# Seven block products over four PSUM banks in a decoder trunk, and memory probabilities in another pool

## The chip, the cores and the metric

The kernel runs on one core of a Trainium2 chip. The metric is the device time of one execution in microseconds (us). Engines: PE (TensorE, matmuls), DVE (VectorE), ACT (ScalarE), POOL (GpSimd) and SP (SyncE, which here only issues DMAs). SBUF is the on-chip memory; PSUM has eight banks, each 128 x 512 float32, which matmuls write.

## The reference

Four decoder layers over 256 tokens of width 1024, all in float32:

```python
def reference(x, mem, ...):
    mem_n = _rmsnorm(mem, g_mem)
    for i in range(DEPTH):                      # DEPTH = 4
        proj = _rmsnorm(x, g_mix[i]) @ w_in[i]  # 1024 -> 3 * 1024 + 256
        cols, mq = proj[..., :3 * MIX_WIDTH], proj[..., 3 * MIX_WIDTH:]
        mix = ...                               # i % 3: stick-breaking attention,
                                                # differential attention, short gated convolution
        mo = _memory_attention(mq, mem_n, w_mem_kv[i])   # 4 heads x 64, 256 memory tokens, softmax
        x = x + jnp.concatenate([mix, mo], axis=-1) @ w_o[i]
        x = x + _swiglu(_rmsnorm(x, g_ffn[i]), w_ffn_in[i], w_ffn_out[i])
    return _rmsnorm(x, g_final)

def _swiglu(x, w_in, w_out):
    gu = x @ w_in                               # 1024 -> 2 * 2816
    return (jax.nn.silu(gu[..., :D_FF]) * gu[..., D_FF:]) @ w_out
```

## The kernel before

All weights (225 MB) are streamed once. The 256 tokens are two tiles of 128 (t = 0, 1). A weight matrix comes in chunks of 128 x 1024 numbers: `wchunk` issues one DMA on SyncE into a *raw* tile (pool `wraw`, 7 tiles), and `wparts` splits it: ACT casts it into `whi` (L131, a shorter float format that PE runs in one pass), and DVE writes what the cast lost into `wlo` (L132). Both live in the pool `wsplit`, eight of each. The tokens are split in the same way (`xth`, `xtl`), so a product is three matmuls, `mm3` (L136 to L138). They have 128 x 128 weights loaded in PE (of the tokens) and 512 moving columns (of the chunk).

`proj` takes a projection of 512 columns: four chunks, for each t 24 matmuls into one PSUM bank, and then an evacuation. `out_proj` does the output projections with four banks. Work that has to follow some time later is put into a list by `later(rounds, f)`, and `flush()`, called in the middle and at the end of each pass over a chunk set, runs what is due. So the Python order of the program weaves the attention of one projection into the matmuls of the next one.

The order on each engine is made by a planner: it takes the instructions by their place in the program, lets one go ahead when what it needs is ready in the planner's own model of the time, and gives out the tiles of a pool. Tiles with one tag share that tag's buffers. At run time each engine follows its list in order and waits on semaphores.

Memory attention (`mem_attention`, one for each layer) runs in `first`, `second` and `third`: `probs(0)` on the first token tile (12 matmuls L383, maximum L386, exponentials L390 on ACT, scaling L394 on DVE), then `turn(0)` (transposes L402, copies L406 and L408) and `probs(1)`, then `turn(1)` and `values`. In layer 0 this lies in the second mixer half's first projection, in the others in the first mixer half's second and third. The probabilities `mprob` (128 x 4 x 256 floats) take a tile of `wraw`, as large as a weight chunk.

The feed-forward input projection has six blocks (b = 0 to 5): gate columns and up columns of 512 each, the last with 256 each. Blocks 0, 2, 3 and 5 are plain `proj` calls. Blocks 1 and 4 use `winograd`: with the tokens (two halves of the width, two token tiles) and the weights (two halves of the rows; gate and up) as 2 x 2 blocks, seven block products take the place of eight. Products 1 and 2 use plain weight and token blocks; 5, 6, 7 and 4 use sums of weight blocks (`plus`, L221 on DVE, `wsum` or in place in a raw tile); 5, 7, 6 and 3 use sums of token blocks, which `tokens_side` makes once for each layer after block 0 (L256 to L262, split in L252 and L253). A product needs four row chunks, two in each of two rounds s = 0, 1. Each of the seven has a PSUM bank of its own through both rounds, and in the second round `h_sums` combines them on DVE (L859 to L873), applies SiLU on ACT (L860, L874) and multiplies gate and up (L852). `hidden` then transposes the result (L836) into the operand `hh`, `hl` of the output projection.

The tag `att` of the pool `work` has NATT = 12 tiles of 128 x 512 floats, for attention, the tokens' sums and the products' sums. `small` has four one-column tiles for each tag.

Of the kernel before, what the change touches and what calls it, by code (L numbers as in the profile page):

```python
# [32 lines left out]
NATT = 12  # L33
# [7 lines left out]
def trunk_kernel(ctx, tc, x, mem, vecs, w_in, w_kv, w_o, w_f1, w_f2, lams, g_final, out):  # L41
# [3 lines left out]
    wraw = pool("wraw", 7)  # L45
# [151 lines left out]
    def winograd(left, right, ab, evac):  # L197
# [99 lines left out]
    def rstd_of(ss, n, scale, eps):  # L297

        r = small.tile([P, n], F32, name="rstd", tag=f"rstd{n}")
        nc.gpsimd.tensor_scalar(r, ss, scale, eps, ALU.mult, ALU.add)  # L300
        nc.gpsimd.tensor_tensor(r, r, nhalf[:, :n], ALU.pow)
        return r

    def stats(src):
        junk = work.tile([P, D], BF16, name="junk", tag="att", bufs=NATT)
        ss = small.tile([P, 1], F32, name="ss", tag="ss")
# [61 lines left out]
    def mem_attention(qT, kv):  # L368
# [5 lines left out]
        def probs(t):  # L374
            prob = wraw.tile([P, 4, S], F32, name="mprob", tag="raw")
            mx = small.tile([P, 4], F32, name="mmx", tag="mmx")
            sm = small.tile([P, 4], F32, name="msm", tag="msm")
# [7 lines left out]
            for r, ps in enumerate(pss):  # L385
                nc.vector.tensor_reduce(mx[:, 2 * r:2 * r + 2], ps, AX.X, ALU.max)  # L386
                nc.vector.tensor_scalar(mx[:, 2 * r:2 * r + 2], mx[:, 2 * r:2 * r + 2], -0.125, None, ALU.mult)
                for pr in range(2):
                    j = 2 * r + pr
                    nc.scalar.activation(prob[:, j, :], ps[:, pr, :], AF.Exp, bias=mx[:, j:j + 1], scale=0.125,  # L390
                                         accum_out=sm[:, j:j + 1])
            nc.vector.reciprocal(sm, sm)
            for j in range(4):
                nc.vector.tensor_scalar(prob[:, j, :], prob[:, j, :], sm[:, j:j + 1], None, ALU.mult)  # L394
            return prob

        def turn(t, prob):
            for j0 in (0, 2):
                tr = ps_x.tile([P, 4, P], F32, name="tr", tag="ps")
                for j in (j0, j0 + 1):  # L400
                    for m in range(NT):
                        nc.tensor.transpose(tr[:, 2 * (j - j0) + m, :], prob[:, j, m * P:(m + 1) * P], ident)  # L402
# [98 lines left out]
    def diff_scores(qT, kT, hh0, lam, res, then):  # L501
        diffs = []
        abias = alibi(hh0)
        for e in range(2):
            bias = abias[:, e]
            mx = small.tile([P, 4], F32, name="dmx", tag="dmx")
            sm = small.tile([P, 4], F32, name="dsm", tag="dsm")
# [36 lines left out]
    def diff_values(aTs, v, c0, oh, ol, ghead):  # L544
        ons = []
        for e in range(2):
# [7 lines left out]
            ss = small.tile([P, 2], F32, name="dss", tag="dss")  # L554
# [35 lines left out]
    def final():  # L590
        gfin = big.tile([P, D], F32, name="gfin", tag="big")
        nc.sync.dma_start(gfin, g_final.partition_broadcast(P))
        ss = [small.tile([P, 2], F32, name="fss", tag="fss") for _ in range(NT)]
# [83 lines left out]
    for i in range(DEPTH):  # L677
# [29 lines left out]
        def q_scale(t):  # L707
            r = small.tile([P, 1], F32, name="rq", tag="rq")
# [105 lines left out]
        for b in range(6):  # L814
# [29 lines left out]
            if b in (1, 4):  # L844
                sums = {}

                def h_sums(p, acc, sums=sums, sg=sg, hh=hh, hl=hl):
                    tt = nc.vector.tensor_tensor
                    new = lambda name: work.tile([P, 512], F32, name=name, tag="att", bufs=NATT)

                    def up(t, c):
                        nc.vector.scalar_tensor_tensor(sg[t], c, rneg[t], sg[t], ALU.mult, ALU.mult)  # L852
                        later(2, lambda: hidden(t, sg[t], hh, hl, 512))

                    if p == 1:
                        sums["v"] = new("sv")
                        nc.scalar.copy(sums["v"], acc[1])
                    elif p == 2:
                        tt(sg[0], acc[2], sums["v"], ALU.add)  # L859
                        nc.scalar.activation(sg[0], sg[0], AF.Silu, scale=rx[0])  # L860
                    elif p == 6:
# [68 lines left out]
```

## Time and profile before

| | |
|---|---|
| median of 3 runs | 1333.34 us (1332.73 to 1334.71) |
| profiled execution: time, span | 1336.26 us, 1334.5 us |
| mean granted TensorE clock in it | 0.986 of full |
| instructions | 16363, of which 6079 matmuls |
| weights read | 225.23 MB, mean 170 GB/s over the span |
| DMAs of feed-forward input weights | 160 of 512 KB, median 4.3 us to landing |

The span is the time from the first to the last instruction; the profiled execution's own time has 1.8 us around it. An instruction's row names the engine, the line, the operation and `out<-in` by the names of the tiles. "[4.41 <-ACT whi L131]" says that the engine had been idle for 4.41 us and that the end of ACT's instruction on `whi` at line 131 released it. Rows of a list of waits read: who waits, for whom, us in total, times, the longest. "x5" merges neighbours of one kind, from the start of the first to the end of the last. SPq is SyncE's issuing of a DMA; PEld is the loading of PE's 128 x 128 operand, which overlaps the matmuls.

### The profile page before, as it was taken

To read this page: it belongs to the slowest core of one execution; us is meant where nothing else is said; L and a number is where in the kernel's file an instruction comes from. 1 tells how busy PE (TensorE), PEld (TensorE's weight loads), DVE (VectorE), ACT (ScalarE), POOL (GpSimd) and SP (SyncE) were. 2 spreads that over 40 slices of the span, in tenths; PEclk is the share of its full clock that TensorE was granted. 3 is DMA by queue.
4 is the path that set the end of the run, shared out by engine and by line. 5 is a ranking of instruction groups with operands and counts; after the bars stand their busy time and mean duration, and the time that the engine had idled before them with its cause. 6 is when DMAs were issued, how large, how long until landed. Compare 5 with 4: busy or idle time off the path is not lost.

```text
span 1334.5 us, 16363 instructions
## 1 busy us (share of the span) xinstructions
PE 1290.3 (97%) x6079; PEld 1056.6 (79%) x6079; DVE 930.3 (70%) x1163; ACT 721.1 (54%) x1015; POOL 60.0 (4%) x109
## 2 busy tenths in 40 slices
PE   9989999999989999999998999999999899999997
PEld 6878887878878888787886888788888688878786
DVE  7645598795647659879464877978744745996952
ACT  7646466564446546656344545656434655664642
POOL 2000000000111000000000000000000001000001
PEclk9989999999999999999998999999999899999999
DMA  9426536477426454747743664475752645364660
GB/s 342 149 74 211 158 112 224 135 226 243 121 84 207 172 158 122 242 124 242 221 126 103 224 196 124 140 240 161 263 171 79 205 142 158 88 213 156 202 224 31
DMA packets 107791, 227.34 MB, mean 170 GB/s; under 512 B 7488, under 2 KB 20288, under 8 KB 107712
## 3 DMA queue, kind: packets, MB, share of 16 engines
q1 hardware_dynamic: 107712, 226.31, 52.9%
q8 instruction: 47, 0.77, 0.2%
q14 instruction: 32, 0.26, 0.1%
HBM read 225.23 MB, written 1.05 MB: 170 GB/s over the span
## 4 chain that ended last, share of the span: by engine, by line
PE 76%; DVE 16%; issue 3%; ACT 2%; DMA 1%; SPq 0%; POOL 0%; POOLq 0%; ACTq 0%; DVEq 0%
PE acc L137 23%; PE acc L138 23%; PE acc L136 23%; DVE wlo L132 7%; DVE wsum L221 2%; ACT whi L131 1%; PE tr L334 1%; DMA raw<-in_w_ffn_out 1%; PE tr L836 1%; PE tr L320 1%; DVE raw L221 1%; DVE sl L253 1%; PE at L415 1%; PE at L449 1%; PE at L491 1%
## 5 line engine op out<-in xcount | busy, mean ns | idle before, releaser
L132 DVE TENSOR_TENSOR wlo<-raw,whi 128x1024 fp32r<-128x1024 f32 (+1 forms) x428 | 510.0, 1209 | 186.1 <-ACT whi L131 183.1
L131 ACT CAST whi<-raw 128x1024 fp32r<-128x1024 f32 (+1 forms) x428 | 436.9, 1042 | 277.0 <-PE acc L138 215.5
L136 PE MATMUL acc<-whi,xth 128*128 128x512 f32 (+1 forms) x992 | 396.5, 400 | 18.0 <-ACT whi L131 17.6
L137 PE MATMUL acc<-wlo,xth 128*128 128x512 f32 (+1 forms) x992 | 388.0, 391 | 13.4 <-DVE wlo L132 13.4
L138 PE MATMUL acc<-whi,xtl 128*128 128x512 f32 (+1 forms) x992 | 385.5, 389 | 0.0
L136 PEld LDWEIGHTS acc<-whi,xth 128*128 128x128 f32 x992 | 189.6, 191 | 56.1 <-ACT whi L131 20.1
L137 PEld LDWEIGHTS acc<-wlo,xth 128*128 128x128 f32 x992 | 189.8, 191 | 54.1 <-DVE wlo L132 20.1
L138 PEld LDWEIGHTS acc<-whi,xtl 128*128 128x128 f32 x992 | 189.6, 191 | 37.8
L136 PE MATMUL acc<-whi,hh 128*128 128x512 f32 x320 | 125.4, 392 | 0.0
L138 PE MATMUL acc<-whi,hl 128*128 128x512 f32 x320 | 124.6, 389 | 0.0
L137 PE MATMUL acc<-wlo,hh 128*128 128x512 f32 x320 | 124.5, 389 | 0.0
L131 ACT CAST whi<-wsum 128x1024 fp32r<-128x1024 f32 x48 | 50.5, 1052 | 55.8 <-DVE wsum L221 52.0
L138 PEld LDWEIGHTS acc<-whi,hl 128*128 128x128 f32 x320 | 60.1, 188 | 12.5
L137 PEld LDWEIGHTS acc<-wlo,hh 128*128 128x128 f32 x320 | 60.1, 188 | 12.2
L136 PEld LDWEIGHTS acc<-whi,hh 128*128 128x128 f32 x320 | 60.1, 188 | 12.2
L132 DVE TENSOR_TENSOR wlo<-wsum,whi 128x1024 fp32r<-128x1024 f32 x48 | 58.5, 1218 | 5.9 <-ACT whi L131 5.5
L137 PE MATMUL acc<-wlo,sh 128*128 128x512 f32 x128 | 50.7, 396 | 0.7
L136 PE MATMUL acc<-whi,oh 128*128 128x512 f32 x128 | 51.1, 399 | 0.0
L138 PE MATMUL acc<-whi,ol 128*128 128x512 f32 x128 | 50.0, 391 | 0.0
L138 PE MATMUL acc<-whi,sl 128*128 128x512 f32 x128 | 49.9, 390 | 0.0
L137 PE MATMUL acc<-wlo,oh 128*128 128x512 f32 x128 | 49.9, 390 | 0.0
L136 PE MATMUL acc<-whi,sh 128*128 128x512 f32 x128 | 49.2, 389 | 0.0
(215 smaller groups left out, 1415.0 us busy)
## 6 DMA issues: line engine op xcount, KB each, us to landing
raw<-in_w_ffn_in SPq DMA_DIRECT2D x160, 512.0 KB, 4.3
raw<-in_w_in SPq DMA_DIRECT2D x100, 512.0 KB, 4.4
raw<-in_w_ffn_out SPq DMA_DIRECT2D x88, 512.0 KB, 4.8
raw<-in_w_o SPq DMA_DIRECT2D x40, 512.0 KB, 4.6
raw<-in_w_mem_kv SPq DMA_DIRECT2D x16, 512.0 KB, 5.4
raw<-in_w_ffn_in SPq DMA_DIRECT2D x32, 256.0 KB, 3.6
raw<-in_w_in SPq DMA_DIRECT2D x8, 256.0 KB, 5.6
x<-in_x SPq DMA_DIRECT2D x4, 256.0 KB, 4.2
```

The source lines that it names most:

```text
L131: nc.scalar.copy(hi, raw)
L132: wlast[:] = [nc.vector.tensor_tensor(lo, raw, hi.bitcast(F32), ALU.subtract)]
L136: nc.tensor.matmul(ps, lh, wh, start=first, stop=False)
L137: nc.tensor.matmul(ps, lh, wl, start=False, stop=False)
L138: return nc.tensor.matmul(ps, ll, wh, start=False, stop=last)
L221: nc.vector.tensor_tensor(out, a, b, ALU.add)
L253: tt(lo, src, hi.bitcast(F32), ALU.subtract)
L320: last_pe = nc.tensor.transpose(ps[:, c, :], src[:, kc * P:(kc + 1) * P], ident).ins
L334: nc.tensor.transpose(ps[:, c, :], src[:, c * P:(c + 1) * P], ident)
L415: nc.tensor.matmul(ps[r * 64:(r + 1) * 64, 0, :], vn[:, m, c:c + 64], pT[2 * r + pr][:, m, :], start=m == 0, stop=m == NT - 1)
L449: nc.tensor.matmul(z[:, 0:2, :], kT[:, h, 0:P], qT[:, h, :], start=True, stop=True)
L491: nc.tensor.matmul(ps[:, 0:2, :], v[0][:, c:c + P], a[h][:, 0:2, :], start=True, stop=False)
```

## The change

Four things change.

1. `winograd` becomes `strassen`. The seven products run in two parts: products 1, 5, 7 and 6 for both rounds, and then 2 for both rounds, and 4 and 3 by turns. They share four banks: 1 and 2, 5 and 3, 7 and 4 accumulate in one bank each, 6 has its own. The sums with 6 and 1 (`u`) and with 7 (`y`) are read off the banks between the two parts. The weight sums of both rounds and the raw chunks b22 are kept until the second part, which also loads b21. `gated` takes over from `h_sums`: the gate half of t = 0 goes from PSUM straight to SiLU, the three others add `u` or `y` to what is in PSUM.
2. `tokens_side` and the negated scales are called between the gate and the up projection of block 0, not after both.
3. `mprob` is two tiles of the tag `att` (2 x 256 floats each) and no longer a raw tile. `wraw` has 8 tiles, `att` 11.
4. Small one-column tiles of several tags share one tag with 14 buffers.

```diff
-NATT = 12
+NATT = 11
...
-    wraw = pool("wraw", 7)
+    wraw = pool("wraw", 8)
...
-    def winograd(left, right, ab, evac):
+    def strassen(left, right, ab, out):
         acc = {}
+        banks = {1: 1, 2: 1, 5: 5, 3: 5, 7: 7, 4: 7, 6: 6}
         def product(p, w, s):
-            if s == 0:
-                acc[p] = ps_acc.tile([P, 512], F32, name="acc", tag="ps")
+            b = banks[p]
+            if b not in acc:
+                acc[b] = ps_acc.tile([P, 512], F32, name="acc", tag="ps")
             lh, ll = ab[p]
             for k in range(2):
                 kc = 2 * s + k
-                mm3(acc[p], lh[:, kc, :], ll[:, kc, :], w[0][:, k, :], w[1][:, k, :], kc == 0, kc == 3)
-            if s == 1:
-                evac(p, acc)
+                start, stop = kc == 0 and p == b, kc == 3
+                nc.tensor.matmul(acc[b], lh[:, kc, :], w[0][:, k, :], start=start, stop=False, skip_group_check=True)
+                nc.tensor.matmul(acc[b], lh[:, kc, :], w[1][:, k, :], start=False, stop=False, skip_group_check=True)
+                nc.tensor.matmul(acc[b], ll[:, kc, :], w[0][:, k, :], start=False, stop=stop, skip_group_check=True)
...
+        part = lambda name: work.tile([P, 512], F32, name=name, tag="att", bufs=NATT)
+        b22, sums = [], []
+        v, u, y = part("sv"), part("su"), part("sy")
         for s in range(2):
             b11, b12 = (load(c, 2 * s * P) for c in (left, right))
-            b21, b22 = (load(c, 512 + 2 * s * P) for c in (left, right))
+            b22.append(load(right, 512 + 2 * s * P))
             product(1, wparts(b11), s)
             t = wraw.tile([P, 2, 512], F32, name="wsum", tag="raw")
             plus(t, b11, b12)
+            if s == 1:
+                nc.scalar.copy(v, acc[1])
             product(5, wparts(t), s)
             flush()
-            product(2, wparts(b21), s)
-            plus(t, t, b22)
+            plus(b12, b12, b22[s])
+            product(7, wparts(b12), s)
+            plus(t, t, b22[s])
             product(6, wparts(t), s)
             flush()
-            plus(b12, b12, b22)
-            product(7, wparts(b12), s)
-            product(3, wparts(b22), s)
+            sums.append(t)
+        plus(u, acc[6], v)
+        plus(y, acc[7], u)
+        b21 = [load(left, 512 + 2 * s * P) for s in range(2)]
+        for s in range(2):
+            product(2, wparts(b21[s]), s)
+        out(0, 0, acc[1], None)
+        out(1, 1, acc[5], y)
+        flush()
+        for s in range(2):
+            plus(sums[s], sums[s], b21[s])
+            product(4, wparts(sums[s]), s)
+            if s == 1:
+                out(1, 0, acc[7], u)
+            product(3, wparts(b22[s]), s)
             flush()
-            plus(t, t, b21)
-            product(4, wparts(t), s)
+        out(0, 1, acc[5], u)
...
-            prob = wraw.tile([P, 4, S], F32, name="mprob", tag="raw")
-            mx = small.tile([P, 4], F32, name="mmx", tag="mmx")
-            sm = small.tile([P, 4], F32, name="msm", tag="msm")
+            probs2 = [work.tile([P, 2, S], F32, name="mprob", tag="att", bufs=NATT) for _ in range(2)]
+            prob = [probs2[j // 2][:, j % 2, :] for j in range(4)]
+            mx = small.tile([P, 4], F32, name="mmx", tag="sm", bufs=14)
+            sm = small.tile([P, 4], F32, name="msm", tag="sm", bufs=14)
...
-                def h_sums(p, acc, sums=sums, sg=sg, hh=hh, hl=hl):
...
+                def gated(t, side, ps, add, sg=sg, hh=hh, hl=hl, up={}):
+                    if side == 0:
+                        src = ps
+                        if add is not None:
+                            nc.vector.tensor_tensor(sg[t], ps, add, ALU.add)
+                            src = sg[t]
+                        nc.scalar.activation(sg[t], src, AF.Silu, scale=rx[t])
+                        up[t, 0] = sg[t]
+                    else:
+                        up[t, 1] = add if t == 1 else work.tile([P, 512], F32, name="sx", tag="att", bufs=NATT)
+                        nc.vector.tensor_tensor(up[t, 1], ps, add, ALU.add)
+                    if (t, 0) in up and (t, 1) in up:
+                        nc.vector.scalar_tensor_tensor(sg[t], up[t, 1], rneg[t], sg[t], ALU.mult, ALU.mult)
                         later(2, lambda: hidden(t, sg[t], hh, hl, 512))
...
-                winograd(gcols, ucols, ab, h_sums)
+                strassen(gcols, ucols, ab, gated)
             elif n == 512:
                 proj([gcols], xT, lambda t, ps: h_out(t, ps, None))
+                if b == 0:
+                    ab, rneg = tokens_side(xg, xT), negative(rx)
                 proj([ucols], xT, lambda t, ps: h_out(t, None, ps))
             else:
                 proj([gcols, ucols], xT, lambda t, ps: h_out(t, ps[:, :n], ps[:, n:2 * n]))
-            if b == 0:
-                ab = tokens_side(xg, xT)
-                rneg = []
...
```

More of the change, by code (lines that the diff above doesn't have):

```diff
@@ L297, in rstd_of @@
     def rstd_of(ss, n, scale, eps):
-        r = small.tile([P, n], F32, name="rstd", tag=f"rstd{n}")
+        r = small.tile([P, n], F32, name="rstd", tag=f"rstd{n}", bufs=4 if n == 1 else 2)
         nc.gpsimd.tensor_scalar(r, ss, scale, eps, ALU.mult, ALU.add)
@@ L305, in stats @@
         junk = work.tile([P, D], BF16, name="junk", tag="att", bufs=NATT)
-        ss = small.tile([P, 1], F32, name="ss", tag="ss")
+        ss = small.tile([P, 1], F32, name="ss", tag="sm", bufs=14)
         nc.scalar.activation(junk, src, AF.Square, accum_out=ss)
@@ L401, in turn @@
                     for m in range(NT):
-                        nc.tensor.transpose(tr[:, 2 * (j - j0) + m, :], prob[:, j, m * P:(m + 1) * P], ident)
+                        nc.tensor.transpose(tr[:, 2 * (j - j0) + m, :], prob[j][:, m * P:(m + 1) * P], ident)
                 for j in (j0, j0 + 1):
@@ L505, in diff_scores @@
             bias = abias[:, e]
-            mx = small.tile([P, 4], F32, name="dmx", tag="dmx")
-            sm = small.tile([P, 4], F32, name="dsm", tag="dsm")
+            mx = small.tile([P, 4], F32, name="dmx", tag="sm", bufs=14)
+            sm = small.tile([P, 4], F32, name="dsm", tag="sm", bufs=14)
             ps = []
@@ L553, in diff_values @@
             on = work.tile([P, NT, 256], F32, name="df_o", tag="qkn", bufs=4)
-            ss = small.tile([P, 2], F32, name="dss", tag="dss")
+            ss = small.tile([P, 2], F32, name="dss", tag="sm", bufs=14)
             for t in range(NT):
@@ L592, in final @@
         nc.sync.dma_start(gfin, g_final.partition_broadcast(P))
-        ss = [small.tile([P, 2], F32, name="fss", tag="fss") for _ in range(NT)]
+        ss = [small.tile([P, 2], F32, name="fss", tag="sm", bufs=14) for _ in range(NT)]
         def evac(t, h, acc):
@@ L707, in q_scale @@
         def q_scale(t):
-            r = small.tile([P, 1], F32, name="rq", tag="rq")
+            r = small.tile([P, 1], F32, name="rq", tag="sm", bufs=14)
             nc.vector.tensor_scalar(r, rx[t], QSCALE, None, ALU.mult)
@@ L844, in trunk_kernel @@
             if b in (1, 4):
-                sums = {}
-                def h_sums(p, acc, sums=sums, sg=sg, hh=hh, hl=hl):
[L848 to L852, printed above, removed]
-                        later(2, lambda: hidden(t, sg[t], hh, hl, 512))
[L855 to L861, printed above, removed]
-                        sums["u"], sums["x"] = new("su"), new("sx")
-                        tt(sums["u"], acc[6], sums["v"], ALU.add)
-                        tt(sums["x"], acc[5], sums["u"], ALU.add)
-                    elif p == 7:
-                        sums["y"] = new("sy")
-                        tt(sums["u"], acc[7], sums["u"], ALU.add)
-                        tt(sums["y"], acc[5], sums["u"], ALU.add)
-                    elif p == 3:
-                        tt(sums["x"], acc[3], sums["x"], ALU.add)
-                        up(0, sums["x"])
-                    elif p == 4:
-                        tt(sg[1], acc[4], sums["u"], ALU.add)
-                        nc.scalar.activation(sg[1], sg[1], AF.Silu, scale=rx[1])
-                        up(1, sums["y"])
@@ L882, in trunk_kernel @@
                 proj([gcols, ucols], xT, lambda t, ps: h_out(t, ps[:, :n], ps[:, n:2 * n]))
-            if b == 0:
-                ab = tokens_side(xg, xT)
-                rneg = []
-                for t in range(NT):
-                    r = small.tile([P, 1], F32, name="rneg", tag="rneg")
-                    nc.vector.tensor_scalar(r, rx[t], -1.0, None, ALU.mult)
-                    rneg.append(r)
         def f_lhs(kc, t):
```

10 lines of the change are left out of this document (8 added, 2 removed).

## The prediction

> **What bounds the kernel now.** I read the page first, for the share of each engine and the chain that ended last.
>
> ```profile
> span 1334.5 us, 16363 instructions
> ...
> PE 1290.3 (97%) x6079; PEld 1056.6 (79%) x6079; DVE 930.3 (70%) x1163; ACT 721.1 (54%) x1015; POOL 60.0 (4%) x109
> ...
> PE 76%; DVE 16%; issue 3%; ACT 2%; DMA 1%; SPq 0%; POOL 0%; POOLq 0%; ACTq 0%; DVEq 0%
> ```
>
> PE is busy for 97% of the span, and the change removes not one matmul. So all that can be won is PE's idle time, 1334.5 - 1290.3 = 44 us, and time in which PE runs at a reduced clock, which counts as busy. The second view is therefore PE's list of waits, with two rows of SyncE's own list beside it.
>
> ```profile
> PE acc L136 <- ACT whi L131: 17.6, 4, 4.4
> PE acc L137 <- DVE wlo L132: 13.4, 21, 1.1
> PE tr L836 <- DVE sg L852: 4.1, 4, 1.0
> SPq L124 <- DVE mprob L394: 77.9, 4, 22.1
> ```
>
> Two kinds of place: four long waits, one in each layer, for a cast of weights; and 25 waits of about 1 us. The third view, the timeline, tells where the long ones are. Here are SyncE, ACT and PE of layer 0, and PE's first matmul after the wait in the last layer.
>
> ```profile
> 48.47 14.02 SPq L124 DMA_DIRECT2D raw<-in_w_in  x5
> 59.79 1.05 ACT L131 CAST whi<-raw 128x1024 fp32r<-128x1024 f32 x1
> 83.43 1.14 DVE L394 TENSOR_SCALAR mprob<-mprob,msm 128x256 f32<-128x256 f32 x4
> 85.18 1.03 PE L402 MATMUL tr<-ident,mprob 128*128 128x128 f32 x8
> 86.24 8.34 SPq L124 DMA_DIRECT2D raw<-in_w_in  x3
> 90.32 0.21 ACT L390 ACTIVATION_READ_ACCUMULATOR mprob<-at,mmx 128x1 f32 x1
> 90.41 5.78 ACT L131 CAST whi<-raw 128x1024 fp32r<-128x1024 f32 x6
> 91.52 0.80 PE L136 MATMUL acc<-whi,xth 128*128 128x512 f32 x1 [4.41 <-ACT whi L131]
> 93.11 0.80 PE L137 MATMUL acc<-wlo,xth 128*128 128x512 f32 x1 [0.36 <-DVE wlo L132]
> 1043.34 0.80 PE L136 MATMUL acc<-whi,xth 128*128 128x512 f32 x1 [4.41 <-ACT whi L131]
> ```
>
> SyncE issues five weight tiles up to 62.5 us and then none until 86.24, when the transposes have freed the first memory-probability tile: two of the seven raw tiles are kept for `mprob`. ACT casts no weights from 60.8 to 90.4 us, and then six tiles without a pause, directly behind the last exponential of the second `probs`. Five of these six had been asked for 28 us or more earlier. So neither the data nor ACT's time was missing; the order written for ACT puts those casts behind the exponentials. In that order raw tiles are handed out as the program asks for them, both `mprob` tiles ahead of the next projection's weights, and the same 4.41 us in the first layer and the last fits a fixed order better than a late transfer. The fourth view, sums by stretch, gives what the wait costs beyond itself.
>
> ```profile
> 62.50:86.20 23.70, 23.70 (x153) 20.76 (x151) 7.00 (x19) 7.94 (x23) 0.81 (x2) 1.00 0.13 39
> 90.98:97.81 6.83, 5.93 (x14) 4.34 (x15) 5.48 (x8) 5.21 (x6) 0.00 (x0) 0.50 0.51 157
> 394.76:401.59 6.83, 5.54 (x13) 4.09 (x14) 5.83 (x9) 5.60 (x6) 0.00 (x0) 0.50 0.46 143
> 725.86:732.69 6.83, 5.99 (x15) 4.73 (x16) 4.66 (x5) 3.93 (x5) 0.00 (x0) 0.50 0.68 217
> 1043.30:1050.13 6.83, 6.43 (x17) 4.68 (x17) 4.97 (x6) 4.71 (x5) 0.00 (x0) 0.50 0.57 180
> ```
>
> Columns: stretch, length, then busy time of PE, PEld, DVE, ACT and POOL, the granted clock, the DMA share and GB/s. In the 23.7 us before the wait, ACT is busy for 7.94 and DVE for 7.00 us, and the DMA engines for 13%: room for everything that is missing later. After each wait PE has half its clock for 6.83 us.
>
> The small waits lie in and behind the blocks with seven products (two in each layer). Sums of the stretches, then DVE and PE at the end of layer 0's first such block, then PE at the end of its second:
>
> ```profile
> 176.80:216.20 39.40, 36.85 (x163) 28.86 (x161) 38.13 (x45) 26.43 (x32) 0.00 (x0) 1.00 0.46 142
> 255.40:288.40 33.00, 32.19 (x149) 26.38 (x147) 28.92 (x31) 21.38 (x24) 0.00 (x0) 1.00 0.53 162
> 210.78 1.21 DVE L132 TENSOR_TENSOR wlo<-wsum,whi 128x1024 fp32r<-128x1024 f32 x1
> 211.91 0.68 DVE L867 TENSOR_TENSOR su<-acc,su 128x512 f32<-128x512 f32 x1
> 212.51 0.68 DVE L870 TENSOR_TENSOR sx<-acc,sx 128x512 f32<-128x512 f32 x1
> 214.97 2.34 DVE L132 TENSOR_TENSOR wlo<-raw,whi 128x1024 fp32r<-128x1024 f32 x2
> 212.04 0.50 PE L137 MATMUL acc<-wlo,xth 128*128 128x512 f32 x1 [0.31 <-DVE wlo L132]
> 214.50 0.66 PE L836 MATMUL tr<-ident,sg 128*128 128x128 f32 x4 [1.03 <-DVE sg L852]
> 216.23 0.50 PE L137 MATMUL acc<-wlo,xth 128*128 128x512 f32 x1 [1.08 <-DVE wlo L132]
> 287.09 0.50 PE L137 MATMUL acc<-wlo,xth 128*128 128x512 f32 x1 [0.81 <-DVE wlo L132]
> 289.73 0.50 PE L137 MATMUL acc<-wlo,xth 128*128 128x512 f32 x1 [0.48 <-DVE wlo L132]
> ```
>
> DVE is busy for 38.13 of 39.40 us around the first block: here it is the bound. Between the split of the last product (210.78) and that of the next block's weights (214.97) it does five sums, 3.06 us, and PE waits. In the second block DVE has some slack (28.92 of 33.00).
>
> **The change part by part.** *Memory probabilities in the work tiles, eight raw tiles.* No instruction is added or removed; two half tiles take the place of one. The weight loads no longer stop behind `mprob`, and the casts of the next projection can be ordered as soon as a split tile is free, in the 23.7 us above. Gone: the four waits, 17.6 us; the short ones behind them, 4 x 0.36 = 1.4 us; and the half clock, half of PE's busy time in the four stretches, (5.93 + 5.54 + 5.99 + 6.43) / 2 = 11.9 us. Together 30.9 us. Its ends are 0 (the casts stay where they are) and 30.9; all three observations above (the stopped queue, the six casts in a row, ACT's idle time) point to the upper end, from which I take off 2 us: casts and splits now lie between exponentials, and the first transposes have little slack (`mprob` is scaled at 83.43 + 1.14 = 84.57, its transposes start at 85.18, while a cast takes 1.05). What comes next there is PE itself. I take -29.
>
> On the clock the Trainium skill (TensorE: Matmul & The Clock Gate, Part 1) says that the clock halves after an idle window of about 3.4 us and returns after a busy one. The stretches of 0.50 behind the 4.41 us waits agree with it; by it a wait that is only cut below 3.4 us would already give the whole 11.9 us back. But two rows in the next part show a reduced clock behind waits of about 1 us, so the trace bears the rule out only in part, and I don't use it in the sum.
>
> *Seven products over four banks.* The matmuls are the same 84 for a block. Eight raw sums and fourteen casts and splits stay too. Of the sums that read PSUM, seven become five: the second product accumulates onto the first in its bank, and the SiLU reads it there; the others add in PSUM where two additions stood. That is 2 x 0.60 us of DVE (the step from 211.91 to 212.51) for a block, 9.6 us for eight. It is worth time only where DVE is the bound: 1.2 of the first blocks' 0.31 + 1.03 + 1.08 = 2.42 us, and about 0.9 of the second blocks' 0.81 to 1.29. That makes at most 4 x 2.1 = 8.4 us. Behind the last split at most four of these operations are left, two of which have to wait for the last product anyway, so the next block's weights come earlier in DVE's order; this is in the 8.4 already, since PE is behind by DVE's total. After the first block the clock is reduced in some layers:
>
> ```profile
> 216.23:220.83 4.60, 4.60 (x15) 3.54 (x15) 4.49 (x5) 3.01 (x5) 0.00 (x0) 0.63 0.80 229
> 548.78:553.38 4.60, 4.60 (x21) 3.75 (x22) 4.60 (x5) 2.80 (x4) 0.00 (x0) 1.00 0.76 207
> ```
>
> That costs 0.37 x 4.60 = 1.7 us in layer 0 and nothing in layer 1. The price on the other side: the shared banks. PE may start the fourth product only when DVE has read the seventh from its bank, and the third only when it has read the fifth. That is a chain of three sums, about 1.9 us, behind the sixth product, against 12 matmuls of the second product (19.60 us hold 86, so 2.7 us) as cover; with one or two splits of 1.14 us (half of the row at 214.97) queued ahead of it, PE waits up to 1.5 us a block, 12 us in all. Two raw sums and two raw tiles are held for the whole block, so six of eight raw tiles are taken while the next block's weights should load; but two tiles are free by the middle, two loads are some 5 us of PE's work, and the eighth raw tile helps. Ends for the products: -13.9 (all the small waits of four layers) and +12. I take -5, nearer to the gain, since total DVE work falls in a stretch that DVE bounds.
>
> *Tokens' sums between the gate and the up half of the first block.* The same eight operations on DVE, 0.6 us each, and four casts; only their place moves, ahead of the third and fourth split of the up half.
>
> ```profile
> 175.03 1.22 DVE L132 TENSOR_TENSOR wlo<-raw,whi 128x1024 fp32r<-128x1024 f32 x1
> 169.00:191.80 22.80, 22.80 (x108) 18.89 (x107) 22.80 (x30) 15.59 (x22) 1.82 (x2) 1.00 0.32 93
> ```
>
> The last split of the up half ends at 176.2 and would end at about 181.0. PE starts that half 48 matmuls after 169.1, at about 180.0, and needs its fourth weights some 4 us later. PE has no idle time in this stretch; cost 0, hidden by the gate half. *Eleven work tiles for twelve, shared small tiles*: the block needs eight for the tokens and three for its sums, and the fourth sum takes a tile that is free again by then: 0.
>
> Sum: -29 - 5 + 0 = -34 us. The profiled execution took 1336.3 us (span 1334.5 and 1.8 around it), 2.9 above the median of 1333.3. So about 1302 for such an execution and 1299 for the median; I say 1300.
>
> **The rivals.** *Half of it (1311 to 1324).* The casts do move, but the work tiles take over the role of the raw tiles, or `turn` waits for probabilities that splits have delayed: a wait of 2 us each at two places in four layers gives back 16 us. For it: 0.6 us of slack at 85.18. Against it: DVE and ACT are two thirds idle there.
>
> *The casts stay (1323 to 1333).* If their place in ACT's order comes from something else than the tiles, the long waits remain, and only the products' 0 to -10 us is left. For it: five of the six tiles were in the memory long before, so it isn't a missing tile at run time. Against it: the same place in all four layers, behind exactly the tile that shared their pool.
>
> *Slower (about 1345).* The shared banks and held tiles: each block gets a stop in its middle. The five sums, 3.06 us, come into PE's path, and loads that find no free raw tile add about 1.5 us; with 1.7 us of reduced clock behind each stop this makes 6.3 us a block and 50 us in all, against 34 + 5 expected without them: 1333 - 34 + 5 + 50 is above 1350, and with part of the clock kept about 1345. It decides from 29 / 8 = 3.6 us a block on.
>
> ```profile
> ACT whi L131 <- DMA raw<-in_w_ffn_in: 12.4, 9, 2.1
> ```
>
> For it speaks that ACT already waits for these loads; against it, that each such wait is at most 2.1 us.
>
> The Trainium skill (PSUM — Partial Sum Buffer, PSUM bank collisions) says that two engines must not use one bank at once and that software has to keep them apart. By this rule the reads are waits for PE rather than overlaps. No run here shows a matmul waiting for a read of its own bank.
>
> **How the numbers follow.** The long waits go and the products cost or gain little: 0.62, 1290 to 1310, median 1300. Half of it: 0.15. The casts stay: 0.11, a little under half of it within 0.2% (2.7 us, about what a measurement can tell from no change). Slower: 0.12. So faster 0.83, same 0.05, slower 0.12. The range reaches from 1289 (all small waits gone as well, 1333.3 - 30.9 - 13.9 = 1288.5) into the cases of half and of no gain, to 1328; what it leaves out is the slower case and part of the one before.
>
> **What would show it.** SyncE's list has no wait for `mprob`; PE's has no 4.4 us wait for `whi`; no stretch of clock 0.50 near the memory attention; casts of the next projection stand between the two `probs`. DVE's sums on PSUM number 16 fewer. If PE's list has new rows of `acc` behind DVE's sums, the banks are at fault; if `tr L402` waits for `mprob`, the slack was too small; casts still behind the exponentials would make the forecast wrong.

## The result

The changed kernel takes 1285.09 us (median of 4 runs, 1284.95 to 1285.19), the kernel before 1333.48 us beside it: a ratio of 0.9636, 95% interval 0.9619 to 0.9653. It is faster by 48.4 us. Forecast were 1300 us, with 1289 to 1328 as the range; the time lies below it. Two single executions in these series, one of the kernel before (1854.2 us) and one of `m_raw8_two` below (2592.9 us), ran far slower than the others of their kernel and are in no median or range.

The page of the changed kernel (span, busy time of the engines, chain that ended last):

```profile
span 1283.2 us, 16324 instructions
...
PE 1270.3 (99%) x6079; PEld 1046.2 (82%) x6079; DVE 923.2 (72%) x1147; ACT 721.4 (56%) x1015; POOL 55.0 (4%) x109
...
PE 91%; DVE 5%; ACT 1%; DMA 1%; issue 1%; SPq 0%; POOL 0%; POOLq 0%; ACTq 0%
```

The same 6079 matmuls keep PE busy for 20.0 us less than before (1290.3), and its idle time falls from 44.2 to 12.9 us. So less than two thirds of the 51.3 us between the two spans is idle time; the rest was hidden in the 97% as slow matmuls. DVE has 16 instructions fewer. PE's list of waits in the changed kernel:

```profile
PE acc L214 <- DVE sy L224: 2.5, 4, 0.7
PE acc L137 <- DVE wlo L132: 1.6, 3, 0.8
...
PE tr L430 <- DVE mprob L422: 0.4, 1, 0.4
```

The 17.6 us for `whi`, most of the 13.4 us for `wlo` and the 4.1 us for `sg` are gone. New is the first row: matmuls that wait for a sum to be read off their bank. SyncE's list has no row for `mprob` any more. ACT in layer 0, where it cast no weights for 30 us before:

```profile
80.48 1.05 ACT L131 CAST whi<-raw 128x1024 fp32r<-128x1024 f32 x1 [1.81 <-PE acc L138]
81.44 0.47 ACT L418 ACTIVATE mprob<-at,mmx 128x256 f32<-128x256 f32 x1
...
83.24 2.00 ACT L131 CAST whi<-raw 128x1024 fp32r<-128x1024 f32 x2
85.13 0.70 ACT L468 ACTIVATE qkn<-acc,rq 128x512 f32<-128x512 f32 x1
85.71 0.39 ACT L436 COPY mpT<-tr 128x256 f32<-128x256 f32 x1
85.97 1.08 ACT L131 CAST whi<-raw 128x1024 fp32r<-128x1024 f32 x1
```

Casts stand around the exponentials now, and no matmul waits for them. Sums by stretch of the changed kernel (columns as before: PE, PEld, DVE, ACT, POOL, granted clock, DMA share, GB/s): the stretch ahead of the former wait, the one around the first product block, and layer 0's whole feed-forward input projection; then that projection in the kernel before.

```profile
62.50:86.20 23.70, 23.70 (x155) 20.77 (x156) 13.86 (x26) 13.50 (x30) 1.64 (x2) 1.00 0.47 143
169.00:208.00 39.00, 39.00 (x177) 31.72 (x177) 38.74 (x43) 29.18 (x35) 0.00 (x0) 1.00 0.54 173
160.63:282.53 121.90, 121.25 (x557) 99.35 (x555) 111.03 (x120) 77.20 (x91) 0.74 (x2) 1.00 0.61 195
```

```profile
168.53:296.73 128.20, 124.33 (x556) 100.38 (x555) 113.88 (x124) 77.39 (x91) 1.82 (x2) 0.99 0.55 171
```

In the first stretch DVE and ACT do almost twice the work that they did there before (7.00 and 7.94 us). The first product block is still one where DVE never rests (38.74 of 39.00), but PE no longer stops in it. The two long rows run from the same matmul to the same matmul (the counts take in one or two that run over the start): 128.20 against 121.90 us, of which 3.2 us is idle time (3.87 against 0.65) and 3.1 us slower matmuls (124.33 against 121.25). Over the four layers such stretches lose 12.0 us of idle time (14.5 to 2.5) and 8.8 us of busy time (493.6 to 484.8).

The spans differ by 51.3 us, and two kinds of stage account for all of it. A layer's mixer runs from the last matmul of the layer before (in layer 0 from the start of the span) up to PE's first matmul on the memory attention's output `om`, its feed-forward input from the last matmul of the output projection (on `ol`) to the first on `hh`; in the changed kernel's layer 0:

```profile
129.10 0.45 PE L136 MATMUL acc<-whi,om 128*128 128x512 f32 x1
...
160.63 0.39 PE L138 MATMUL acc<-whi,ol 128*128 128x512 f32 x1
...
282.53 0.39 PE L136 MATMUL acc<-whi,hh 128*128 128x512 f32 x1
```

Over four layers, from such rows, the mixers fall from 454.4 to 424.0 us (-30.4) and the feed-forward input projections from 508.2 to 487.3 us (-20.9). The medians differ by 2.9 us less than the spans, since the profiled execution of before stood that much above its median.

### The profile page after: what moved, and what is told of

It reads as the page before. It is cut to its first block, busy times and chain, and to the rows that moved or that the text cites. A ratio compares the mean times of both kernels' runs of the same rounds, so it can differ in the third digit from the quotient of the medians.

```text
span 1283.2 us, 16324 instructions
## 1 busy us (share of the span) xinstructions
PE 1270.3 (99%) x6079; PEld 1046.2 (82%) x6079; DVE 923.2 (72%) x1147; ACT 721.4 (56%) x1015; POOL 55.0 (4%) x109
## 4 chain that ended last, share of the span: by engine, by line
PE 91%; DVE 5%; ACT 1%; DMA 1%; issue 1%; SPq 0%; POOL 0%; POOLq 0%; ACTq 0%
PE acc L136 25%; PE acc L138 25%; PE acc L137 25%; PE acc L214 3%; DVE wlo L132 3%; PE acc L215 3%; PE acc L216 3%; PE tr L864 1%; PE tr L361 1%; PE tr L347 1%; DVE wsum L224 1%; ACT whi L131 1%; PE tr L430 1%; DMA raw<-in_w_ffn_out 1%; PE at L411 1%
## 5 line engine op out<-in xcount | busy, mean ns | idle before, releaser
L136 PE MATMUL acc<-whi,xth 128*128 128x512 f32 (+1 forms) x896 | 353.5, 395 | 0.1
L137 PE MATMUL acc<-wlo,xth 128*128 128x512 f32 (+1 forms) x896 | 342.8, 383 | 1.6 <-DVE wlo L132 1.6
L138 PE MATMUL acc<-whi,xtl 128*128 128x512 f32 (+1 forms) x896 | 343.8, 384 | 0.0
L138 PEld LDWEIGHTS acc<-whi,xtl 128*128 128x128 f32 x896 | 168.4, 188 | 33.8
L137 PEld LDWEIGHTS acc<-wlo,xth 128*128 128x128 f32 x896 | 168.9, 188 | 32.6 <-DVE wlo L132 2.8
L136 PEld LDWEIGHTS acc<-whi,xth 128*128 128x128 f32 x896 | 168.6, 188 | 31.5 <-issue 0.8
L136 PEld LDWEIGHTS acc<-whi,hh 128*128 128x128 f32 x320 | 60.1, 188 | 12.1
L214 PE MATMUL acc<-whi,sh 128*128 128x512 f32 x128 | 51.0, 399 | 0.0
```

What stands on the lines that cost most here:

```text
L136: nc.tensor.matmul(ps, lh, wh, start=first, stop=False)
L137: nc.tensor.matmul(ps, lh, wl, start=False, stop=False)
L138: return nc.tensor.matmul(ps, ll, wh, start=False, stop=last)
L214: nc.tensor.matmul(acc[b], lh[:, kc, :], w[0][:, k, :], start=start, stop=False, skip_group_check=True)
```

## Experiments

All times in us. "Mixers" and "ffn in" are the sums over four layers just explained, from each kernel's trace, good to 0.1 us.

| kernel | median (range) | ratio to before, 95% interval | mixers | ffn in |
|---|---|---|---|---|
| before | 1333.5 | 1 | 454.4 | 508.2 |
| changed | 1285.09 | 0.9636 [0.9619, 0.9653] | 424.0 | 487.3 |
| `m_only` | 1306.51 (1305.58-1307.27) | 0.9789 [0.9774, 0.9803] | 424.9 | 507.1 |
| `raw8_only` | 1333.55 (1327.53-1334.46) | 0.9988 [0.9975, 1.0001] | 452.3 | 501.9 |
| `m_raw8` | 1303.55 (1301.63-1306.44) | 0.9768 [0.9749, 0.9788] | 424.3 | 504.3 |
| `p_only` | 1326.90 (1325.76-1328.25) | 0.9940 [0.9923, 0.9957] | 452.7 | 501.3 |
| `a_raw7` | 1301.12 (1300.50-1301.31) | 0.9755 [0.9740, 0.9770] | 424.3 | 503.0 |
| `a_mraw` | 1313.43 (1312.45-1314.32) | 0.9848 [0.9833, 0.9863] | 452.2 | 487.2 |
| `a_toklate` | 1284.03 (1283.39-1284.91) | 0.9628 [0.9614, 0.9642] | 424.7 | 485.7 |
| `a_latesums` | 1300.54 (1300.10-1302.31) | 0.9751 [0.9734, 0.9767] | 424.9 | 502.5 |
| `a_onesum` | 1288.46 (1288.30-1288.55) | 0.9662 [0.9645, 0.9678] | 424.2 | 490.7 |
| `m_raw8_late` | 1304.66 (1303.80-1305.24) | 0.9782 [0.9768, 0.9797] | 424.3 | 505.3 |
| `m_raw8_two` | 1290.12 (1289.91-1290.33) | 0.9674 [0.9658, 0.9690] | 424.2 | 492.4 |
| `m_raw8_one` | 1286.66 (1286.28-1286.72) | 0.9646 [0.9626, 0.9666] | 424.2 | 488.0 |
| `a_banks7` | 1281.44 (1281.35-1281.52) | 0.9608 [0.9592, 0.9624] | 424.0 | 483.7 |
| `a_banks6` | 1280.19 (1280.08-1280.87) | 0.9600 [0.9586, 0.9615] | 424.4 | 481.9 |
| `b7_toklate` | 1279.71 (1279.24-1281.40) | 0.9598 [0.9584, 0.9612] | 424.2 | 482.0 |

The trace of `raw8_only` is of a run of 1328.6 us, at the low end of its range, that of `m_raw8_two` of another run of the same kernel (1290.18 us).

**The probabilities.** `m_only` is the kernel before with this part alone:

```diff
-            prob = wraw.tile([P, 4, S], F32, name="mprob", tag="raw")
+            probs2 = [work.tile([P, 2, S], F32, name="mprob", tag="att", bufs=NATT) for _ in range(2)]
+            prob = [probs2[j // 2][:, j % 2, :] for j in range(4)]
...
```

> Only the memory probabilities move, into two work tiles; seven raw tiles, twelve work tiles and the old products stay. Theory (the planner hands out raw tiles in program order, so the next projection's casts were ordered behind the second probs): the four 4.41 us waits and the four stretches of half clock go, the mixers lose 30.4 us as in the changed kernel, the feed-forward parts keep their waits: 1303 us (1301 to 1305). Rival (the eighth raw tile did it): 1318 us or more. Rival (the gain needs both halves of the change): about 1333 us.

`raw8_only` gives the kernel before one more raw tile and leaves the probabilities where they were (`wraw` 8, `NATT = 11`, shared small tiles). 

> The kernel before with eight raw tiles for seven and eleven work tiles for twelve (and the shared small tiles that make room for it); memory probabilities stay in a raw tile. Theory (order, not shortage): the 4.41 us waits stay in all four layers, 1328 to 1334 us, with at most 6 us of gain in the feed-forward parts. Rival (too few raw tiles): a third of the mixers' 30.4 us or more goes, 1323 us or less.

`a_mraw` is the changed kernel with the `-` line above in place of the `+` lines. 

> The changed kernel with the memory probabilities back in one raw tile; eight raw tiles and the new products stay. Theory (order by pool): the four waits of about 4.4 us and the half clock come back, 1285 + 30 = 1315 us (1312 to 1318). Rival (shortage, which eight tiles relieve): 1285 to 1305 us.

`m_only` wins 27.4 us, nearly all in the mixers, and ends 1.5 us above the range of its theory. PE's first row of waits in `raw8_only`, and PE's and SyncE's rows in `a_mraw`:

```profile
PE acc L136 <- ACT whi L131: 17.6, 4, 4.4
```

```profile
PE acc L136 <- ACT whi L131: 17.6, 4, 4.4
...
SPq L124 <- DVE mprob L421: 77.9, 4, 22.1
```

With the probabilities in the raw pool the four waits of 4.4 us stay to the tenth, with eight tiles as with seven. So it is not a lack of tiles at run time but the pool that the probabilities are in; that the pool acts through the order of ACT's list is read from the casts in the timelines, which follow the exponentials without a pause. `a_mraw` loses 28.3 us against the changed kernel, all in the mixers (452.2), and keeps its feed-forward time (487.2). So this part is one cause, and the two gains add.

**The products and the eighth tile.** `m_raw8` is `m_only` with the three edits of `raw8_only`; `p_only` is the kernel before with `strassen` and `gated` alone (seven raw tiles, and the shared small tiles, which stay); `a_raw7` is the changed kernel with `wraw` at 7; `a_toklate` calls `tokens_side` and `negative` after block 0, as before.

> Memory probabilities in work tiles and eight raw tiles, eleven work tiles, with the old seven-bank products and late tokens' sums. Theory: 30.4 us from the mixers and little from the feed-forward parts: 1300 to 1304 us. Rival (the eighth raw tile gives the feed-forward gain): 1285 to 1293 us, and the raw sums of the first seven-product block start during the output projection.

> Only the products in two parts over four banks; memory probabilities stay in a raw tile, seven raw tiles, twelve work tiles, tokens' sums after the whole first block as before. Theory (the 20.9 us of the feed-forward parts come from DVE work that leaves the stretch it bounds: two PSUM sums fewer in each block, and two raw sums that are made during the output projection before): most of it, 1313 to 1317 us, the four 4.41 us waits stay. Rival (the eighth raw tile or the free raw queue gave the feed-forward gain): 1324 to 1330 us. Rival (the early tokens' sums gave it): 1325 us.

> The changed kernel with seven raw tiles for eight. Theory (two raw sums can be made during the output projection because the first three chunks and a free tile are there, which the eighth tile allows): the first seven-product block loses about 2.3 us of lead in each layer and the waits return in part, 1288 to 1295 us. Rival (the fewer PSUM sums and the order alone carry it): 1285 to 1287 us.

> The changed kernel with the tokens' sums and negated scales after the whole first block, as before. Theory (the sums' place changes neither DVE's work nor the bound): same, 1284 to 1287 us. Rival (the early place gives DVE its lead): 1290 us or more, with waits for wlo behind the first seven-product block.

The eighth tile without the products is worth 3 us at most (1306.5 to 1303.6, with ranges that overlap); the products with seven tiles are worth 7 us alone and 5.4 us on top of `m_only` (1306.5 to 1301.1). Both together bring 21.4 us: some 13 us come only from the pair. The late tokens' sums are 1.1 us faster than the early ones, under the 0.2% that can be told apart. My expectations for `p_only` (1313 to 1317) and `a_raw7` (1288 to 1295) gave the products too much: the first met the range of its rival, that the eighth tile or the free raw queue gives the gain, the second lies above both of its ranges.

What does the pair do? DVE's raw weight sums of layer 0's first block in the kernel before, and then in the changed one, where the output projection ends at 160.63 us (rows above):

```profile
176.83 1.21 DVE L221 TENSOR_TENSOR wsum<-raw 128x1024 f32<-128x1024 f32 x1
188.57 1.21 DVE L221 TENSOR_TENSOR raw<-raw 128x1024 f32<-128x1024 f32 x1
```

```profile
151.55 1.22 DVE L224 TENSOR_TENSOR wsum<-raw 128x1024 f32<-128x1024 f32 x1
153.29 1.22 DVE L224 TENSOR_TENSOR raw<-raw 128x1024 f32<-128x1024 f32 x1
```

In the changed kernel b11 + b12 and b12 + b22 are made during the output projection, a stage ahead, where DVE idles; in `a_raw7` they come at 169.77 and 176.79, in `m_raw8` at 169.09 and 180.83. `a_latesums` takes just that away: both sums are ordered behind the last split that stands before the block (`behind`).

```diff
+        behind = wlast[0].ins
...
-            plus(t, b11, b12)
+            with tc.issue_after(behind):
+                plus(t, b11, b12)
...
-            plus(b12, b12, b22[s])
+            with tc.issue_after(behind):
+                plus(b12, b12, b22[s])
```

> The changed kernel (1285.1 us), but in each product block the two raw weight sums t = b11 + b12 and b12 + b22 of the first round are ordered on DVE behind the last weight split that stands before the block, so they can no longer be made during the output projection. Eight raw tiles and the new order of products stay. Theory: the eighth raw tile brings its time by letting DVE make these sums where it idles; then the time goes to that of seven raw tiles, 1296 to 1302 us (+11 to +17 us), the first blocks' feed-forward input projections take about 125.5 us for 121.8, and PE waits again for wlo. Rival: the eighth tile works through earlier loads and casts, not through the sums: 1285 to 1288 us.

`a_onesum` holds back the second sum alone (the last of the two edits). 

> The changed kernel (1285.1 us) with only the second of the two early sums, b12 + b22, ordered behind the last split before the block; t = b11 + b12 stays in the output projection. With both held back it took 1300.5 us. If each sum is worth its share, about 1293 us (1291 to 1295). If one is enough to take DVE out of PE's way, 1285 to 1288 us; if both are needed, 1298 to 1301 us.

With both held back, 15.5 of the 16.0 us that lie between `a_raw7` and the changed kernel are lost, with eight tiles in place; with one held back, 3.4 us, just above the range in which one early sum is enough. The edit acts on more than the two sums: it holds those of the second blocks too, and in the first blocks the sum b11 + b12 of the second round comes later with them (185.16 us for 169.50 in layer 0). DVE in the first block of `a_latesums`, its sums and the only two rows with idle time ahead of them, and then PE's list of waits:

```profile
170.60 1.22 DVE L224 TENSOR_TENSOR wsum<-raw 128x1024 f32<-128x1024 f32 x1
177.62 1.22 DVE L224 TENSOR_TENSOR raw<-raw 128x1024 f32<-128x1024 f32 x1
...
194.43 1.23 DVE L132 TENSOR_TENSOR wlo<-wsum,whi 128x1024 fp32r<-128x1024 f32 x1 [1.12 <-ACT whi L131]
...
204.29 1.23 DVE L132 TENSOR_TENSOR wlo<-wsum,whi 128x1024 fp32r<-128x1024 f32 x1 [1.17 <-ACT whi L131]
```

```profile
PE acc L214 <- DVE sy L224: 4.9, 8, 0.9
PE acc L214 <- ACT whi L131: 4.0, 8, 0.6
PE acc L137 <- DVE wlo L132: 3.1, 5, 0.8
```

A weight sum heads a chain: sum on DVE, cast on ACT, split on DVE, matmuls. Late by 2.4 us of sums, DVE reaches the later sums without a lead, and then waits itself for the casts that its own sums hold up (1.12 and 1.17 us). The expected time came, but the expected wait for `wlo` is only a part of it (3.1 us); PE waits longer for casts (4.0 us) and at the shared banks (4.9 us). The first blocks' stretch in the changed kernel and in `a_latesums`, from PE's first matmul on a token sum (`sh`) to the last before the next block:

```profile
185.40:203.60 18.20, 18.20 (x82) 14.69 (x81) 18.17 (x19) 12.68 (x15) 0.00 (x0) 1.00 0.59 181
```

```profile
186.50:208.00 21.50, 19.63 (x84) 14.75 (x83) 19.21 (x20) 13.41 (x16) 0.00 (x0) 1.00 0.56 157
```

That is 3.3 us of the 3.9 that the whole projection of layer 0 loses, for 2.4 us of moved sums. Of it 1.87 us is idle time; the matmuls take longer too (19.63 us for 84, against 18.20 for 82).

**Is it the two parts, or the order of the loads?** The second raw sum needs b22, which the kernel before loads fourth and the changed kernel third. Three kernels keep the seven banks and the old order of products and change `m_raw8` in the order of the loads, one of them in the place of the second sum too. `m_raw8_late` loads b21 and b22 behind the sum t; `m_raw8_two`:

```diff
-            b21, b22 = (load(c, 512 + 2 * s * P) for c in (left, right))
+            b22 = load(right, 512 + 2 * s * P)
             product(1, wparts(b11), s)
...
             plus(t, b11, b12)
+            plus(b12, b12, b22)
+            b21 = load(left, 512 + 2 * s * P)
...
-            plus(b12, b12, b22)
```

`m_raw8_one` is the same without the added `plus`; b12 + b22 stays behind the sixth product.

> The kernel before with probabilities in the work tiles and eight raw tiles (that kernel took 1303.6 us), seven banks and the old order of products; the one edit is that the loads of b21 and b22 are asked for behind the sum t = b11 + b12, so that this sum stands four raw tiles after the block's start at most and can be made in the output projection. Theory (early sums give the time, two for a first block in the changed kernel, one here): 1296 to 1301 us. Rival (only the products in two parts give it): 1302 to 1305 us.

> The kernel with probabilities in the work tiles and eight raw tiles (1303.6 us), seven banks and the old order of products; the edit lets both first raw sums of a block, t = b11 + b12 and b12 + b22, stand early: b22 is loaded ahead of them and b21 behind them, so that in the first blocks DVE makes both during the output projection, as in the changed kernel. One early sum alone had left this kernel at 1304.7 us. Theory A (two early sums are what counts, whatever the order of products): 1288 to 1294 us. Theory B (they are worth time only with the two parts, where the closing sums no longer stand between PE and the next block; here the four waits of about 1 us behind each block's closing stay): 1300 to 1304 us.

> The same kernel as with both early raw sums in the old order of products (1290.2 us), for its profile. Theory A made right by the time (both sums early, order of products without weight): PE's list of waits has fewer than half of the 20 waits for wlo (11.9 us) that stand with probabilities in the work tiles alone, and the first blocks' feed-forward input projections are some 3 us shorter, about 123 us.

> As the kernel with both early raw sums in the old order of products (1290.2 us), but b12 + b22 is asked for in its old place, behind the sixth product; the order of the loads (b22 ahead of the sum t, b21 behind it) stays. It tells whether one early sum is enough in the old order too, once b22 is loaded early: then 1291 to 1295 us, as in the changed kernel, where one sum early gave 12 of 15.5 us. Rival (in the old order both sums are needed): 1301 to 1305 us, as with both of the later loads behind the sum.

Loading b22 third and b21 fourth brings 13.4 and 16.9 us in the old order of products: theory A, and `m_raw8_one` comes within 1.6 us of the changed kernel with nothing of its parts and banks. In `m_raw8_two` a layer's projection takes 123 us, as theory A had it; ten of the 20 waits for `wlo` that `m_only` has are left (6.2 us), where fewer than half were expected. `m_raw8_one` is faster than the 1291 to 1295 us expected, but it doesn't tell one sum from two. Its DVE makes both early all the same:

```profile
151.82 1.22 DVE L221 TENSOR_TENSOR wsum<-raw 128x1024 f32<-128x1024 f32 x1
153.56 1.21 DVE L221 TENSOR_TENSOR raw<-raw 128x1024 f32<-128x1024 f32 x1
```

In `m_raw8_late`, where only t is early (150.09) and the other sum comes at 169.15, nothing is won, and its theory (1296 to 1301) failed. PE's waits at the end of its first block, and the only one there in `m_raw8_one`:

```profile
203.52 0.50 PE L137 MATMUL acc<-wlo,xth 128*128 128x512 f32 x1 [0.31 <-DVE wlo L132]
...
205.97 0.66 PE L837 MATMUL tr<-ident,sg 128*128 128x128 f32 x4 [1.03 <-DVE sg L853]
...
207.70 0.50 PE L137 MATMUL acc<-wlo,xth 128*128 128x512 f32 x1 [1.07 <-DVE wlo L132]
```

```profile
208.19 0.50 PE L137 MATMUL acc<-wlo,xth 128*128 128x512 f32 x1 [0.81 <-DVE wlo L132]
```

The three waits are those of the kernel before. Why one early sum is worth 12.1 us in the changed kernel (`a_latesums` to `a_onesum`) and nothing here, and why `m_raw8_one` beats `m_raw8_two` by 3.5 us, stays open. In `a_onesum` the two sums stand nearly where they stand in `m_raw8_late` (151.76 and 169.72 us), yet the feed-forward stages take 490.7 against 505.3 us; so the place of these two sums alone doesn't set the time. The planner also placed the last products and splits of these blocks in another order, in `a_latesums` too, and I didn't separate that.

**The shared banks.** `a_banks7` gives each product its own bank (`banks = {p: p for p in range(1, 8)}`), with seven sums on PSUM again; in `a_banks6` only 1 and 2 share:

```diff
-        banks = {1: 1, 2: 1, 5: 5, 3: 5, 7: 7, 4: 7, 6: 6}
+        banks = {1: 1, 2: 1, 5: 5, 3: 3, 7: 7, 4: 4, 6: 6}
...
-        out(1, 1, acc[5], y)
+        plus(v, acc[5], u)
+        plus(u, acc[5], y)
+        out(1, 1, None, u)
...
```

`b7_toklate` is `a_banks7` with the tokens' sums late.

> The changed kernel with a PSUM bank for each of the seven products and seven sums read from PSUM in each block (as before), in the new order. Theory (the fewer PSUM sums are 1.2 us of DVE work in a stretch that DVE bounds): 2 to 9 us slower, 1287 to 1294 us. Rival (only the order and the early raw sums matter): 1285 to 1286 us. Rival (shared banks cost PE waits that separate banks save, 2.5 us in its list): up to 2.5 us faster.

> The changed kernel, but products 3 and 4 have banks of their own (six in use); only products 1 and 2 share one. Products 5 and 7 are then added by DVE in one operation more for each, so six sums on PSUM for a block. If the waits of the fourth and third product for their bank are the cost of sharing (four waits of 0.62 to 0.65 us and what follows from them), it is as fast as with seven banks: 1281 to 1283 us. If the cost comes from the second product on the first one's bank, 1284.5 to 1287 us.

> The changed kernel with a bank for each of the seven products (that one took 1281.4 us) and the tokens' sums after both projections of the first feed-forward block, as before. Made of the two edits that each gained something alone (3.65 and 1.06 us). Theory, that they add: 1279.8 to 1281.0 us. Rival, that the late sums gain only where the shared banks stop PE: 1281 to 1283 us.

Seven banks are 3.65 us faster than four, in spite of 16 more sums: my theory had them slower, and the rival allowed 2.5 us. The two intervals overlap by a little, but the projection is 0.8 to 1.0 us shorter in each of the four layers. PE's list of waits in `a_banks7` has no row of `L214` left:

```profile
PE acc L137 <- DVE wlo L132: 1.3, 3, 0.8
PE warm_ps L62 <- DVE warm L57: 1.2, 1, 1.2
PE tr L432 <- DVE mprob L424: 0.4, 1, 0.4
```

`a_banks6` is as fast (0.8 us faster than its range), so what costs is that products 3 and 4 share a bank with 5 and 7, whose values DVE must read first; accumulating the second product onto the first costs nothing. The best times are 1279.71 (`b7_toklate`) and 1280.19 (`a_banks6`); their intervals overlap. Both beat the changed kernel by about 5 us. `b7_toklate` and `m_raw8_one` both have seven banks, late tokens' sums and b22 loaded third, and differ in the main by the products in two parts, with b21 loaded in the second: some 7 us, which is about what the two parts bring here with separate banks.

## Why the forecast was wrong, step by step

*Mixers: -29 forecast, -30.4 measured.* Right, with its mechanism: the waits, the stopped queue and the half clock are gone together, and the gain comes close to the upper end of the working (30.9). `a_mraw` and `raw8_only` show that it is the pool and not the number of its tiles. The 2 us taken off were not needed: one wait of 0.4 us for `mprob` is what the small slack cost.

*Products: -5 forecast, -20.9 measured.* This is the term that failed, and its upper end (-13.9) too. Two steps did it. First, "eight raw sums and fourteen casts and splits stay too": they stay in number, but two of the eight leave the stretch that DVE bounds. I saw the DVE-bound first block, counted only the operations removed from it (1.2 us a block), and took the eighth raw tile for a cover of late loads. That tile, with b22 loaded ahead of b21, lets two sums of 1.2 us move to a stage where DVE idles; with the early sums held back (`a_latesums`) 15.5 us are lost. The change then takes 1300.5 us, and the feed-forward stages win 5.7 us for the 5 forecast; that this meets 1300 to half a microsecond is partly luck. Second, the upper end was made of listed waits alone. PE's idle time in these stages fell by 12.0 us, which it would have covered, but their busy time fell by 8.8 us as well, which no list of waits shows. Some 3.4 us of that is half clock behind the first blocks of layers 0 and 3; the working had priced it at 1.7 us in layer 0 and not added it. None of the rivals came: each looked for what could take the gain away, none for what could add to it.

*Two readings of the working.* Of its two rows behind the first block only one shows a reduced clock (0.63; the other has 1.00). Half of the row at 214.97 is 1.17 us, not 1.14. Neither changes the sum.

*The sums on PSUM.* 16 fewer, as said, and worth less than they cost: the kernels with seven or six banks do more of them and are faster. The price of the shared banks, up to 1.5 us a block forecast, is 0.46 us a block (3.65 / 8, net of the sums saved) and is listed as four waits of about 0.6 us, in the second block of each layer. The rival that got slower by it needed 3.6 us a block. The Trainium skill (PSUM — Partial Sum Buffer, PSUM bank collisions raise a hardware error) says that software must keep two engines off one bank. The row of `L214` behind `sy`, 2.5 us in four waits, is such a wait; but here the data ask for it too, since the fourth product adds onto values that DVE has still to read, so these runs don't test the rule.

*Tokens' sums: 0 forecast.* 1.1 us slower than at their old place, not to be told from 0. *Work tiles, small tiles: 0.* No row of waits names them.

## What to carry to other kernels

A tile that lives long doesn't belong in a pool that feeds a stream if tiles are handed out in program order: here it held back not only loads but the casts behind it, and one tile more didn't help. Where an engine bounds a stage, look at which of its operations have their data early and what the engine does in the stage before; here holding back the early sums, 2.4 us in each first block, cost 3.8 us a layer (those of the second blocks were held too). Each heads a chain across two engines, which is the likely reason that it is more than their length. And take the upper bound of a gain from what the stage takes at full rate, not from the list of waits.

## What the hardware showed

Half clock behind short waits is decided not by the waits alone but by where they fall. In layer 1, `m_raw8` and `m_only` have the same three waits behind the first block (0.31, 1.03, then 1.07 and 1.08 us). The first matmul after them in `m_raw8`, and in `m_only`:

```profile
531.00 0.79 PE L137 MATMUL acc<-wlo,xth 128*128 128x512 f32 x1 [1.07 <-DVE wlo L132]
```

```profile
532.88 0.50 PE L137 MATMUL acc<-wlo,xth 128*128 128x512 f32 x1 [1.08 <-DVE wlo L132]
```

The clock changes on a grid. In the kernel before, half clock begins at 90.98, 217.27, 394.76, 725.86, 1043.30 and 1186.66 us: from one to the next 37, 52, 97, 93 and 42 times 3.413 us. In all 17 traces with a clock on record every change lies on such a grid, within 0.003 us; where the grid starts differs from trace to trace (the first change comes 4.6 to 6.8 us after the start of the span). Two steps of the grid in `m_raw8`, and two in `m_only`:

```profile
527.28:530.69 3.41, 1.61 (x9) 0.85 (x7) 3.41 (x6) 2.33 (x3) 0.00 (x0) 1.00 0.80 288
530.69:534.11 3.41, 3.11 (x7) 2.48 (x8) 3.12 (x4) 2.58 (x4) 0.00 (x0) 0.50 0.58 166
```

```profile
527.76:531.17 3.41, 2.07 (x9) 1.07 (x7) 3.41 (x6) 1.56 (x3) 0.00 (x0) 1.00 0.92 299
531.17:534.59 3.41, 2.34 (x11) 1.82 (x12) 2.99 (x4) 3.10 (x5) 0.00 (x0) 1.00 0.53 140
```

In `m_raw8` one step holds 1.80 us without a matmul (3.41 - 1.61), and the next has half the clock. In `m_only` the grid parts the same waits into 1.34 and 1.07 us, and the clock stays. By PE's rows in these traces, all 21 steps at full clock with more than 1.74 us of idle time were followed by half clock, none with less than 1.70, and three of the five between: the clock turned where about half of a step was idle. In the kernel before, the first blocks lie on this edge: 1.72, 1.69, 1.71 and 1.74 us in the four layers, with half clock behind the first and the last. The Trainium skill (TensorE: Matmul & The Clock Gate, Part 1) has the clock halve after an idle window of about 3.4 us. The step of the grid has that length, but half of it idle, in waits of at most 1.08 us, was enough here; by that, a wait of 4.41 us cut to just below 3.4 us would most likely still have cost the clock, since one of the two steps that it touches would be about half idle or more.
